# Attention pipelines whose TensorE order is written out, with the scores of two 64-row heads alternated

## The chip, the cores and the metric

The kernel runs on one core of a Trainium2 chip. The metric is device time in microseconds, the median of several executions of the whole program. Times inside the program come from one further execution, taken with the hardware profiler.

## The reference

Two transformer blocks of two layers each work on the same 512 tokens of width 1024, batch 1, in float32.

The first block, in each of its two layers, adds three branches: a multi-scale pooling branch, a gated causal convolution, and a dilated attention of 12 heads of width 64 in three dilation groups; then memory cross-attention and a gated feed-forward part. The second block has 256 context tokens beside the 512. Its first layer holds eight sliding-window heads of width 64 (two key heads, a sink each) and four differential heads, each with two softmaxes over queries and keys of width 64; its second layer is latent attention with 16 heads of 64 + 32 columns. A feed-forward part follows each. What matters here are the scores: a softmax over `q @ k.T` with 64 rows of contraction for the dilated, differential and window heads and 96 for the latent ones, its product with the values, and the projections from which q, k and v come.

```
sc = jnp.einsum("bhqd,bhqkd->bhqk", qb[g], kk).astype(jnp.float32) * scale   # dilated, hd = 64
p = jnp.exp(sc - m); o = jnp.einsum("bhqk,bhqkd->bhqd", p, vv) / den
```

## The kernel before

Float32 products are made of three matmuls on a high and a low part (`mm3`, lines 133 to 138: high by high, high by low, low by high); the lines 136, 137 and 138 therefore hold most matmuls of the program. `wload` (line 123) loads a weight unit with a DMA on the SP queue and splits it: ScalarE copies the high part (line 109), VectorE subtracts the low one (line 112).

Attention is done by `pipeline` (line 382), which is called three times: by `mix1` for the dilated heads (once in each layer of the first block), by `mix_ab` for the differential and then the window heads, and by `mix_mla` for the latent heads. A pipeline has items; an item is one head for one block of 128 queries and has four steps:

- `qk`: the scores of 128 queries against up to 768 columns into one of two PSUM buffers `S`, and their extreme value on VectorE (`nmax`, line 399, or 401 with a mask). The score matrix is negated, so the minimum is taken.
- `soft`: the exponential on ScalarE with the sum beside it (`exps`, line 411), the reciprocal on VectorE (416), and the scaling on GpSimd (`norm_probs`, 420). Differential heads combine two such results on VectorE (1061).
- `tr`: `probs_T` (line 422) transposes the probabilities on TensorE (line 430), three 128-column groups into each of two PSUM tiles `T`, of which there are two buffers; ScalarE copies the first tile out (109), VectorE the second (433).
- `pv`: the product with the values into a PSUM tile `p` (two buffers): `pv_pair` (line 444) for two heads of 64 columns at once, or line 1068 for a differential head.

`pipeline` emits, in each round i, step s of item i - steps[s], in the order `qk`, `tr`, `soft`, `pv`, and then filler. Filler (`Fill`, line 40) is a list of generators that emit other work in small steps and tell what each step should cost in nanoseconds; `run(ns)` hands out steps until the debt is paid, and stops at a tile's boundary when less than `hold` is left; `need(key)` runs everything up to that key at once. In `mix1` the filler is, in this order: the projections of the second pair of heads (`proj1`), the pooling branch's projections (`pool_in`, line 564, with a chain of sums on GpSimd in lines 576 and 578 and on VectorE in 584 to 586 behind each tile), the convolution branch (`conv_branch`, line 542) and the pooling branch's output (`pool_out`, line 591, which reads those sums). In `mix_ab` it is the projections `proj_ab` (line 1029) of the following heads; in `mix_mla` those of the following head group.

The program's instructions are ordered by the language's scheduler, which gives each engine the ready instruction that was emitted first, by its own idea of durations; the order on TensorE need not be that of the source. A projection (`tok_proj`, line 355) ends with copies by ScalarE, rotary steps on VectorE (lines 458 to 461, or `rope2`) and transposes (line 469, or `transposed`, line 1024) through the PSUM tiles `p`, each group of which is emptied by a ScalarE copy and a VectorE subtraction (line 120).

Two heads lie in one tile: rows 0 to 63 hold one, rows 64 to 127 the other. `items1` (dilated heads) has 16 items per layer, `diff_items` eight items per head, of which each pair shares a query block, and two context items, `window_items` 40, and the latent pipeline 64.

Of the kernel before, what the change touches and what calls it, by code (L numbers as in the profile page):

```python
# [39 lines left out]
class Fill:  # L40
# [28 lines left out]
    def drain(self):  # L69
        while self.gens:  # L70
            self._one()
# [7 lines left out]
class Net:  # L79
# [53 lines left out]
    def mm3(self, ps, l, r, first, last):  # L133

        mm = self.nc.tensor.matmul
        mm(ps, lhsT=l[0], rhs=r[0], start=first, stop=False)  # L136
        mm(ps, lhsT=l[0], rhs=r[1], start=False, stop=False)  # L137
        mm(ps, lhsT=l[1], rhs=r[0], start=False, stop=last)  # L138

    def gain(self, row):  # L140
        g = self.gp.tile([P, D], F32, name="g")
# [238 lines left out]


    def pipeline(self, items, fill, ns, steps=(0, 1, 2, 3)):
        for i in range(len(items) + steps[-1]):
            for s in (0, 2, 1, 3):
                j = i - steps[s]
                if 0 <= j < len(items) and items[j][s] is not None:
                    items[j][s]()
            fill.run(ns if isinstance(ns, (int, float)) else ns[min(i, len(items) - 1)])

    def ptile(self):  # L390
        self.turn = (self.turn + 1) % 6
# [83 lines left out]
        g["v"] = vt = self.work.tile([P, 4, 384], F32, name="vt", bufs=2)  # L475
        yield from self.tok_proj(hT, W[l, p, 2], range(4), 384, lambda t, ps: self.copy(vt[:, t], ps), tags=tags)

    def items1(self, p, g, fill, oT):

        mm = self.nc.tensor.matmul  # L480
        sh = {}
        out = []

        def item(b, h):
            st = {}
            rows = slice(64 * h, 64 * h + 64)
            qs = slice(b * P, (b + 1) * P)

            def qk():
                if (b, h) == (0, 0):  # L490
                    fill.need(p)
                q0, k0, q12, k12 = g["q0"], g["k0"], g["q12"], g["k12"]
                ps = self.psum("S")
                self.mm3(ps[:, 0], (q0[rows, 0, qs], q0[rows, 1, qs]), (k0[rows, 0], k0[rows, 1]), True, True)
                for j in range(2):
                    o = ps[:, 1, j * P : (j + 1) * P]
                    mm(o, lhsT=q12[rows, j, qs], rhs=k12[rows, j, qs], start=True, stop=True)
                st["s"] = ps.rearrange("p a b -> p (a b)")[:, :768]
                st["nm"] = self.nmax(st["s"], mask=self.mask1[:, b])

            def soft():
                st["P"], r = self.exps(st["s"], st["nm"], 768)
                self.norm_probs(st["P"], r)

            def tr():
                sh[b, h] = self.probs_T(st["P"], 6)

            def pv():
                v = g["v"]
                o = self.psum("p")[:, :P]  # L510

                def vs(hh, k):
                    c = hh * 64 + (max(k - 3, 0)) * P
                    return v[:, k if k < 4 else b, c : c + 64]

                self.pv_pair(o, [sh[b, 0], sh[b, 1]], vs)
                self.copy(oT[:, qs], o)

            return (qk, soft, tr, pv if h else None)

        return [item(b, h) for b in range(4) for h in range(2)]

    def shifts(self, dst, src, k):

# [87 lines left out]
    def mix1(self, l, hT, lead):  # L612
        nc, I = self.nc, self.I
        with ExitStack() as ctx:
            cf = ExitStack()
            with ExitStack() as c2:
                if l > 0:
                    self.ringctx.close()
                self.psum_pools(c2, S=2, T=2, p=2)
                if l == 0:  # L620
                    self.ready(1)
                    self.rope1()
                    self.consts1()
# [12 lines left out]
                self.masks1(self.pool(c2, "mask"))  # L636
                fp = self.pool(cf, "brf", 8, side="right")
                oF, aF, bF = ([fp.tile([P, 512], F32, name="brf") for _ in range(n)] for n in (2, 3, 3))
                fill.add(1, self.proj1(l, 1, hT, gs[1], ("p",)))
                fill.add("pool", self.pool_in(l, hT, pooled))  # L640
                fill.add("conv", self.conv_branch(l, hT, bF))
                fill.add("pool", self.pool_out(l, pooled, aF))
                self.pipeline(self.items1(0, gs[0], fill, oF[0]) + self.items1(1, gs[1], fill, oF[1]), fill, 7200, (0, 1, 2, 3))
                fill.drain()
            self.open_ring()
            mp = self.pool(ctx, "mT", KC)
# [401 lines left out]
            yield from self.transposed(src, col, range(4), g[n], s, tag=tags[-1])  # L1048
        g["v"] = v

    def diff_items(self, h, g, fill, oB):
# [20 lines left out]
        def item(t, m, first):  # L1072
            st = {}
            rows = slice(64 * m, 64 * m + 64)
            q = slice(t * P, (t + 1) * P)

            def qk():
                if first:
                    fill.need(h)
                qT, kT = g["a"], g["b"]  # L1080
                ql = (qT[rows, 0, q], qT[rows, 1, q])
                ps = self.psum("S")
                self.mm3(ps[:, 0], ql, (kT[rows, 0, :512], kT[rows, 1, :512]), True, True)
                self.mm3(ps[:, 1, :256], ql, (kT[rows, 0, 512:], kT[rows, 1, 512:]), True, True)
                st["s"] = ps.rearrange("p a b -> p (a b)")[:, :768]
                st["nm"] = self.nmax(st["s"])

            def soft():
                sh.setdefault(t, []).append(self.exps(st["s"], st["nm"], 768))
                if m:  # L1090
                    combine(t)

            def tr():
                sh["T", t] = self.probs_T(sh[t][0][0], 6)

            return (qk, soft, tr if m else None, (lambda: finish(t, 6)) if m else None)

        def ctx_item(t):
            st = {}
            q = slice(t * P, (t + 1) * P)  # L1100

            def qk():
                qT, kT = g["a"], g["b"]
# [12 lines left out]
            def tr():  # L1116
                sh["T", t] = self.probs_T(sh[t][0][0], 2)

            return (qk, soft, tr, lambda: finish(t, 2))

        return [item(t, m, t == 0 and m == 0) for t in range(4) for m in range(2)] + [ctx_item(t) for t in (4, 5)]

    def diff_T(self, oB, oT):

# [103 lines left out]
    def mix_ab(self, hT, lead):  # L1228
        nc, I = self.nc, self.I
        with ExitStack() as ctx:  # L1230
            with ExitStack() as c2:
# [34 lines left out]
            self.open_x(back)  # L1266
            self.open_xc()
# [444 lines left out]
```

## Time and profile before

| | us |
|---|---|
| median of 3 runs (lowest to highest) | 3593.13 (3589.31 to 3593.2) |
| the profiled execution | 3594.31 |
| its span in the trace | 3592.5 |
| TensorE busy in the span | 3519.9 (98%) |
| VectorE busy | 1917.2 (53%) |
| ScalarE busy | 1335.5 (37%) |
| GpSimd busy | 429.1 (12%) |
| DMA queue q1, share of 16 engines' span | 31.7% |
| pipeline of the dilated heads, first layer | 72.9 to 250.1 |
| pipeline of the dilated heads, second layer | 998.5 to 1175.9 |
| differential heads, then window heads | 1903.4 to 2231.4 |
| latent heads | 2948.4 to 3173.5 |

The trace names the engines PE (TensorE matmuls), PEld (its weight loads), DVE (VectorE), ACT (ScalarE), POOL (GpSimd) and SP (SyncE, which issues the DMAs). A matmul's duration reaches beyond the start of the next one, since they are pipelined; what a matmul costs is the distance between starts. `64*128` in a row is 64 rows by 128 columns of the array. A float32 matmul that is not split stands as two instructions. In a row's end, [x <-E tile line] is idle time of the engine before the instruction and what ended it.

### The profile page before, as it was taken

The numbers are of one execution on the slowest core, as the hardware profiler recorded it, in microseconds if no ns is written. First come the engines' busy times: TensorE is split into PE (matmuls) and PEld (weight loads), VectorE is DVE, ScalarE is ACT, GpSimd is POOL, SyncE is SP. The second block draws the span as 40 slices with busy tenths as digits, with TensorE's granted clock in tenths as the row PEclk, the third lists the DMA queues.
The fourth block names the chain that finished last, engine by engine and source line by source line (L and its number), as shares of the span: only waits on it lengthen the run. The fifth ranks groups of instructions, "written<-read, shape, count | busy, mean of one in ns | idle before, by whom it ended". The sixth has DMA issues, their size and how long they took to land.

```text
span 3592.5 us, 48260 instructions
## 1 busy us (share of the span) xinstructions
PE 3519.9 (98%) x19261; PEld 2994.1 (83%) x19261; DVE 1917.2 (53%) x3018; ACT 1335.5 (37%) x2372; POOL 429.1 (12%) x572
## 2 busy tenths in 40 slices
PE   8999999999999999999999999999999989999998
PEld 8877798888898778888878887888888878888887
DVE  4453357466534335666766666536663466753243
ACT  4432344332443324532344446332111356643222
POOL 0211111000102111200011122200000122220001
PEclk9999999999999999999999999999999999999999
DMA  4233334344322433354431112335443121022232
GB/s 129 83 129 94 100 112 141 106 144 135 103 66 93 135 94 124 121 167 150 131 107 40 36 48 77 125 93 168 132 132 103 46 80 33 25 89 87 90 102 86
DMA packets 110130, 364.02 MB, mean 101 GB/s; under 512 B 16617, under 2 KB 18209, under 8 KB 109905
## 3 DMA queue, kind: packets, MB, share of 16 engines
q1 hardware_dynamic: 109904, 360.94, 31.7%
q8 instruction: 151, 2.47, 0.3%
q14 instruction: 75, 0.61, 0.1%
HBM read 347.16 MB, written 13.73 MB: 100 GB/s over the span
## 4 chain that ended last, share of the span: by engine, by line
PE 90%; DVE 3%; ACT 2%; POOL 2%; DMA 1%; issue 1%; SPq 0%; ACTq 0%; POOLq 0%; DVEq 0%
PE ps L136 21%; PE ps L137 21%; PE ps L138 21%; PE p L136 4%; PE p L137 4%; PE p L138 4%; PE T L430 3%; PE p L444 3%; PE S L136 2%; PE S L137 1%; PE S L138 1%; DMA adaw<-in_ada_w_dram 1%; PE T L138 1%; PE T L136 1%; PE T L137 1%
## 5 line engine op out<-in xcount | busy, mean ns | idle before, releaser
L112 DVE TENSOR_TENSOR wlo<-raw,whi 128x1024 fp32r<-128x1024 f32 (+2 forms) x510 | 603.8, 1190 | 734.6 <-ACT whi L109 719.3
L109 ACT ACTIVATE whi<-raw 128x1024 fp32r<-128x1024 f32 (+2 forms) x510 | 518.1, 1019 | 1113.1 <-PE ps L137 710.2
L137 PE MATMUL ps<-hTlo,whi 128*128 128x512 f32 (+1 forms) x2048 | 757.6, 370 | 4.1 <-DVE hTlo L177 4.0
L136 PE MATMUL ps<-hThi,whi 128*128 128x512 f32 (+1 forms) x2048 | 757.7, 371 | 2.7 <-ACT hThi L109 1.4
L138 PE MATMUL ps<-hThi,wlo 128*128 128x512 f32 (+1 forms) x2048 | 756.7, 370 | 0.0
L136 PEld LDWEIGHTS ps<-hThi,whi 128*128 128x128 f32 x2048 | 385.8, 189 | 73.0 <-issue 3.5
L137 PEld LDWEIGHTS ps<-hTlo,whi 128*128 128x128 f32 x2048 | 386.5, 189 | 69.9 <-DVE hTlo L177 4.5
L138 PEld LDWEIGHTS ps<-hThi,wlo 128*128 128x128 f32 x2048 | 386.3, 189 | 65.2
L930 DVE SCALAR_TENSOR_TENSOR acc<-adaw,cs,acc 128x1024 f32<-128x1024 f32 x168 | 209.4, 1279 | 14.6 <-DMA adaw<-in_ada_w_dram 14.3
L136 PE MATMUL ps<-whi,a 128*128 128x512 f32 x440 | 170.9, 392 | 0.7 <-ACT a L109 0.7
L138 PE MATMUL ps<-whi,a 128*128 128x512 f32 x440 | 170.6, 390 | 0.0
L137 PE MATMUL ps<-wlo,a 128*128 128x512 f32 x440 | 170.6, 390 | 0.0
L136 PE MATMUL p<-whi,hThi 128*128 128x384 f32 x464 | 163.1, 352 | 7.5 <-ACT hThi L175 3.1
L137 PE MATMUL p<-wlo,hThi 128*128 128x384 f32 x464 | 158.2, 341 | 4.7 <-DVE wlo L112 4.7
L154 POOL TENSOR_SCALAR rstd<-ms 128x1 f32<-128x1 f32 x78 | 24.1, 309 | 1137.9 <-ACT junk L152 1122.7
L138 PE MATMUL p<-whi,hTlo 128*128 128x384 f32 x464 | 158.2, 341 | 0.7 <-DVE hTlo L112 0.7
L262 DVE TENSOR_TENSOR y<-y,ps 128x1024 f32<-128x1024 f32 x88 | 106.6, 1218 | 85.7 <-PE ps L138 85.4
L136 PE MATMUL ps<-whi,act 128*128 128x512 f32 x352 | 138.2, 395 | 0.0
L137 PE MATMUL ps<-wlo,act 128*128 128x512 f32 x352 | 137.2, 392 | 0.0
L138 PE MATMUL ps<-whi,act 128*128 128x512 f32 x352 | 136.3, 390 | 0.0
L420 POOL TENSOR_SCALAR g<-g,den 128x768 f32<-128x768 f32 (+3 forms) x88 | 74.6, 850 | 424.3 <-DVE den L416 375.6
L109 ACT ACTIVATE PT<-T 128x384 f32<-128x384 f32 (+2 forms) x160 | 74.4, 465 | 111.6 <-PE T L430 109.6
(407 smaller groups left out, 6830.8 us busy)
## 6 DMA issues: line engine op xcount, KB each, us to landing
raw<-in_ffn_w_dram SPq DMA_DIRECT2D x132, 512.0 KB
adaw<-in_ada_w_dram SPq DMA_DIRECT2D x96, 512.0 KB
raw<-in_w_up_dram SPq DMA_DIRECT2D x88, 512.0 KB
raw<-in_w_gate_dram SPq DMA_DIRECT2D x48, 512.0 KB
raw<-in_w_down_dram SPq DMA_DIRECT2D x44, 512.0 KB
raw<-in_w_qkv_dram SPq DMA_DIRECT2D x48, 384.0 KB
xd<-x SPq DMA_DIRECT2D x20, 512.0 KB
raw<-in_w_conv_dram SPq DMA_DIRECT2D x18, 512.0 KB
```

What stands on the lines that cost most here:

```text
L109: return self.nc.scalar.activation(out, in_, AF.Copy, scale=scale)
L112: return self.nc.vector.tensor_tensor(out, a, b, op=ALU.subtract)
L136: mm(ps, lhsT=l[0], rhs=r[0], start=first, stop=False)
L137: mm(ps, lhsT=l[0], rhs=r[1], start=False, stop=False)
L138: mm(ps, lhsT=l[1], rhs=r[0], start=False, stop=last)
L154: nc.gpsimd.tensor_scalar(r, ms, 1.0, EPS, op0=ALU.mult, op1=ALU.add)
L262: self.nc.vector.tensor_tensor(yps[t], yps[t], y, op=ALU.add)
L420: self.nc.gpsimd.tensor_scalar(Pt, Pt, r, 1.0, op0=ALU.mult, op1=ALU.mult)
L430: nc.tensor.transpose(ps[:, k * P : (k + 1) * P], Pt[:, (k0 + k) * P : (k0 + k + 1) * P], self.ident)
L444: self.nc.tensor.matmul(o[64 * h : 64 * h + 64], lhsT=vs(h, k), rhs=PTs[h][:, k], start=k == 0, stop=k == nk - 1)
L930: nc.vector.scalar_tensor_tensor(acc[r], w, c, acc[r], op0=ALU.mult, op1=ALU.add)
```

## The change

`pipeline` puts TensorE under a manual schedule: inside it, TensorE takes its instructions in the order in which the source emits them. The other engines are scheduled as before. The order in a round becomes `pv`, `qk`, `tr`, `soft`, then filler, and an item may bring its own step offsets. In `items1` and `diff_items`, the two heads of a tile become one item: their score matmuls are given out alternately (`mm3_two`), each head into its own `S` buffer, and then come two extremes, two exponentials and, in `items1`, 12 transposes in a row. In `mix1` the order of the filler becomes convolution, `pool_in`, `pool_out`; the second pair's projections are no filler any more but are emitted in one piece ahead of its first scores. In `mix_ab`, a head's projections are added to the filler only when the head before it begins. Window and latent items keep their steps.

```diff
+    def mm3_two(self, pss, ls, rs):
+        for i, j in ((0, 0), (0, 1), (1, 0)):
+            for ps, l, r in zip(pss, ls, rs):
+                self.nc.tensor.matmul(ps, lhsT=l[i], rhs=r[j], start=(i, j) == (0, 0), stop=i == 1)
...
     def pipeline(self, items, fill, ns, steps=(0, 1, 2, 3)):
-        for i in range(len(items) + steps[-1]):
-            for s in (0, 2, 1, 3):
-                j = i - steps[s]
-                if 0 <= j < len(items) and items[j][s] is not None:
-                    items[j][s]()
-            fill.run(ns if isinstance(ns, (int, float)) else ns[min(i, len(items) - 1)])
+        own = [it[4] if len(it) > 4 else steps for it in items]
+        with self.tc.manual_schedule(engines={mybir.EngineType.PE}):
+            for i in range(max(j + o[3] for j, o in enumerate(own)) + 1):
+                for s in (3, 0, 2, 1):
+                    for j, it in enumerate(items):
+                        if j + own[j][s] == i and it[s] is not None:
+                            it[s]()
+                fill.run(ns if isinstance(ns, (int, float)) else ns[min(i, len(items) - 1)])
...
-    def items1(self, p, g, fill, oT):
+    def items1(self, p, g, proj, oT):
...
             def qk():
-                if (b, h) == (0, 0):
-                    fill.need(p)
+                if b == 0 and p:
+                    drain(proj)
                 q0, k0, q12, k12 = g["q0"], g["k0"], g["q12"], g["k12"]
-                ps = self.psum("S")
-                self.mm3(ps[:, 0], (q0[rows, 0, qs], q0[rows, 1, qs]), (k0[rows, 0], k0[rows, 1]), True, True)
+                pss = [self.psum("S") for _ in both]
+                self.mm3_two([ps[:, 0] for ps in pss], [(q0[r, 0, qs], q0[r, 1, qs]) for r in both], [(k0[r, 0], k0[r, 1]) for r in both])
                 for j in range(2):
-                    o = ps[:, 1, j * P : (j + 1) * P]
-                    mm(o, lhsT=q12[rows, j, qs], rhs=k12[rows, j, qs], start=True, stop=True)
+                    for ps, r in zip(pss, both):
+                        mm(ps[:, 1, j * P : (j + 1) * P], lhsT=q12[r, j, qs], rhs=k12[r, j, qs], start=True, stop=True)
...
             def tr():
-                sh[b, h] = self.probs_T(st["P"], 6)
+                sh[b] = [self.probs_T(Pt, 6) for Pt in st["P"]]
...
-        return [item(b, h) for b in range(4) for h in range(2)]
+        return [item(b) for b in range(4)]
...
-                fill.add(1, self.proj1(l, 1, hT, gs[1], ("p",)))
+                proj = self.proj1(l, 1, hT, gs[1], ("p",))
+                fill.add("conv", self.conv_branch(l, hT, bF))
                 fill.add("pool", self.pool_in(l, hT, pooled))
-                fill.add("conv", self.conv_branch(l, hT, bF))
                 fill.add("pool", self.pool_out(l, pooled, aF))
-                self.pipeline(self.items1(0, gs[0], fill, oF[0]) + self.items1(1, gs[1], fill, oF[1]), fill, 7200, (0, 1, 2, 3))
+                items = self.items1(0, gs[0], None, oF[0]) + self.items1(1, gs[1], proj, oF[1])
+                self.pipeline(items, fill, [9000] * 4 + [8500] * 4, (0, 0, 1, 2))
...
             def qk():
-                if first:
+                if t == 0:
                     fill.need(h)
+                    fill.add(*after)
                 qT, kT = g["a"], g["b"]
...
+                pss = [self.psum("S") for _ in both]
+                for j, c, n in ((0, slice(0, 512), 512), (1, slice(512, 768), 256)):
+                    self.mm3_two([ps[:, j, :n] for ps in pss], ql, [(kT[r, 0, c], kT[r, 1, c]) for r in both])
...
-            return (qk, soft, tr if m else None, (lambda: finish(t, 6)) if m else None)
+            return (qk, soft, tr, lambda: finish(t, 6), (0, 0, 2, 3))
...
-                for i in range(1, 6):
-                    fill.add(i, self.proj_ab(hT, i, gs[i], ("p",)))
+                proj = [(i, self.proj_ab(hT, i, gs[i], ("p",))) for i in range(1, 6)]
                 items = []
                 for h in range(4):
-                    items += self.diff_items(h, gs[h], fill, oB[h])
+                    items += self.diff_items(h, gs[h], fill, oB[h], proj[h])
+                qk5 = items[-1][0]
+
+                def last():
+                    qk5()
+                    fill.add(*proj[4])
+
+                items[-1] = (last,) + items[-1][1:]
...
-                self.pipeline(items, fill, [3000] * n + [200] * (len(items) - n), (0, 1, 4, 5))
+                self.pipeline(items, fill, ([6000] * 4 + [3000] * 2) * 4 + [200] * (len(items) - n), (0, 1, 4, 5))
```

## Rows read from the trace of the kernel before

**Rows 1.** Windows view of four stretches: bounds, length, busy us (instructions) per engine, PEclk, DMA.

```profile
72.90:250.10 177.20, 174.46 (x1022) 148.59 (x1021) 79.70 (x159) 69.55 (x119) 32.03 (x44) 0.99 0.29 92
...
1903.40:2137.20 233.80, 229.25 (x1374) 203.59 (x1375) 148.07 (x365) 95.72 (x242) 38.19 (x67) 1.00 0.14 44
2137.20:2231.40 94.20, 92.58 (x750) 71.91 (x749) 67.08 (x257) 63.49 (x204) 33.09 (x54) 1.00 0.06 17
2948.40:3173.50 225.10, 222.04 (x1902) 195.11 (x1900) 157.93 (x333) 146.59 (x316) 60.03 (x64) 1.00 0.11 34
```

**Rows 2.** Timeline of TensorE around a lone head: start us, us, engine, line, operation, tiles, count.

```profile
1912.99 0.33 PE L137 MATMUL p<-wlo,hThi 128*128 128x384 f32 x1
1913.16 0.34 PE L138 MATMUL p<-whi,hTlo 128*128 128x384 f32 x1
1913.43 0.49 PE L136 MATMUL S<-qk 64*128 64x512 f32 x1
...
1914.67 0.44 PE L136 MATMUL p<-whi,hThi 128*128 128x384 f32 x1
1914.95 0.34 PE L137 MATMUL p<-wlo,hThi 128*128 128x384 f32 x1
```

**Rows 3.** Timeline of TensorE, two runs of six 256-column score matmuls.

```profile
1942.95 0.39 PE L136 MATMUL S<-qk 64*128 64x256 f32 x2
...
1943.51 0.60 PE L1068 MATMUL p<-v,PT 128*128 128x128 f32 x3
...
2142.27 0.38 PE L136 MATMUL S<-qk 64*128 64x256 f32 x1
...
2143.18 0.44 PE L430 MATMUL T<-ident,g 128*128 128x128 f32 x2
```

**Rows 4.** Timeline of TensorE, a head cut by two transposes.

```profile
97.88 0.39 PE L137 MATMUL S<-qk 64*128 64x512 f32 x1
98.20 0.44 PE L469 MATMUL p<-ident,tok 128*128 128x128 f32 x2
98.57 0.49 PE L138 MATMUL S<-qk 64*128 64x512 f32 x1
```

**Rows 5.** Timeline of all engines, three places with two T tiles or two maxima.

```profile
175.71 0.96 DVE L401 CUSTOM_DVE_ANT_0 S<-S,mask 128x768 f32<-128x768 f32 x1
...
1947.25 0.44 PE L430 MATMUL T<-ident,big 128*128 128x128 f32 x2 [0.56 <-ACT PT L109]
...
2130.38 0.73 DVE L401 CUSTOM_DVE_ANT_0 S<-S,mask 128x512 f32<-128x512 f32 x1
...
2132.20 0.55 DVE L433 COPY PT<-T 128x384 f32<-128x384 f32 x1
```

**Rows 6.** Timeline of all engines, the sums behind the last pool matmul.

```profile
173.62 0.69 DVE L112 TENSOR_TENSOR qk<-t,qk 128x512 fp32r<-128x512 f32 x1 [0.70 <-ACT qk L109]
...
174.44 0.57 ACT L109 ACTIVATE t<-p 128x512 f32<-128x512 f32 x1
...
182.21 0.75 DVE L586 SCALAR_TENSOR_TENSOR t<-t,poolc,t 128x512 f32<-128x512 f32 x1
```

**Rows 7.** Timeline of all engines, rotary steps of a projection tile.

```profile
106.69 0.49 ACT L109 ACTIVATE tok<-p 128x384 f32<-128x384 f32 x1 [4.61 <-PE p L138]
...
107.82 0.26 DVE L461 TENSOR_TENSOR tok<-ropeA,ropeB 128x96 f32<-128x96 f32 x1
```

**Rows 8.** Timeline of all engines, value products at the latent pipeline's end.

```profile
3164.68 1.53 PE L444 MATMUL p<-PT,v 128*64 128x128 f32 x24
...
3170.78 0.49 ACT L109 ACTIVATE PT<-T 128x384 f32<-128x384 f32 x1 [0.24 <-PE T L430]
...
3170.95 1.89 PE L444 MATMUL p<-PT,v 128*64 128x128 f32 x24
```

**Rows 9.** Windows view, a stall in the first layer and the stretch behind it.

```profile
126.00:129.00 3.00, 1.82 (x13) 1.40 (x11) 2.88 (x7) 1.99 (x5) 1.73 (x1) 1.00 0.31 42
129.02:132.43 3.41, 3.41 (x12) 3.03 (x12) 0.71 (x3) 1.62 (x4) 0.94 (x2) 0.50 0.28 115
```

More of the change, by code (lines that the diff above doesn't have):

```diff
@@ L482, in items1, with item @@
         out = []
-        def item(b, h):
+        def item(b):
             st = {}
-            rows = slice(64 * h, 64 * h + 64)
+            both = [slice(0, 64), slice(64, 128)]
             qs = slice(b * P, (b + 1) * P)
             def qk():
-                if (b, h) == (0, 0):
-                    fill.need(p)
+                if b == 0 and p:
+                    drain(proj)
                 q0, k0, q12, k12 = g["q0"], g["k0"], g["q12"], g["k12"]
-                ps = self.psum("S")
-                self.mm3(ps[:, 0], (q0[rows, 0, qs], q0[rows, 1, qs]), (k0[rows, 0], k0[rows, 1]), True, True)
+                pss = [self.psum("S") for _ in both]
+                self.mm3_two([ps[:, 0] for ps in pss], [(q0[r, 0, qs], q0[r, 1, qs]) for r in both], [(k0[r, 0], k0[r, 1]) for r in both])
                 for j in range(2):
-                    o = ps[:, 1, j * P : (j + 1) * P]
-                    mm(o, lhsT=q12[rows, j, qs], rhs=k12[rows, j, qs], start=True, stop=True)
-                st["s"] = ps.rearrange("p a b -> p (a b)")[:, :768]
-                st["nm"] = self.nmax(st["s"], mask=self.mask1[:, b])
+                    for ps, r in zip(pss, both):
+                        mm(ps[:, 1, j * P : (j + 1) * P], lhsT=q12[r, j, qs], rhs=k12[r, j, qs], start=True, stop=True)
+                st["s"] = [ps.rearrange("p a b -> p (a b)")[:, :768] for ps in pss]
+                st["nm"] = [self.nmax(s, mask=self.mask1[:, b]) for s in st["s"]]
             def soft():
-                st["P"], r = self.exps(st["s"], st["nm"], 768)
-                self.norm_probs(st["P"], r)
+                st["P"] = []
+                for s, nm in zip(st["s"], st["nm"]):
+                    Pt, r = self.exps(s, nm, 768)
+                    self.norm_probs(Pt, r)
+                    st["P"].append(Pt)
             def tr():
-                sh[b, h] = self.probs_T(st["P"], 6)
+                sh[b] = [self.probs_T(Pt, 6) for Pt in st["P"]]
             def pv():
@@ L514, in vs @@
                     return v[:, k if k < 4 else b, c : c + 64]
-                self.pv_pair(o, [sh[b, 0], sh[b, 1]], vs)
+                self.pv_pair(o, sh[b], vs)
                 self.copy(oT[:, qs], o)
-            return (qk, soft, tr, pv if h else None)
-        return [item(b, h) for b in range(4) for h in range(2)]
+            return (qk, soft, tr, pv)
+        return [item(b) for b in range(4)]
     def shifts(self, dst, src, k):
@@ L1049, in proj_ab, with diff_items @@
         g["v"] = v
-    def diff_items(self, h, g, fill, oB):
+    def diff_items(self, h, g, fill, oB, after):
         nc = self.nc
@@ L1070, in finish, with item @@
             nc.vector.scalar_tensor_tensor(oB[:, t], o, r, self.subln, op0=ALU.mult, op1=ALU.mult)
-        def item(t, m, first):
+        def item(t):
             st = {}
-            rows = slice(64 * m, 64 * m + 64)
+            both = [slice(0, 64), slice(64, 128)]
             q = slice(t * P, (t + 1) * P)
             def qk():
-                if first:
+                if t == 0:
                     fill.need(h)
+                    fill.add(*after)
                 qT, kT = g["a"], g["b"]
[L1081 to L1086, printed above, removed]
+                ql = [(qT[r, 0, q], qT[r, 1, q]) for r in both]
+                pss = [self.psum("S") for _ in both]
+                for j, c, n in ((0, slice(0, 512), 512), (1, slice(512, 768), 256)):
+                    self.mm3_two([ps[:, j, :n] for ps in pss], ql, [(kT[r, 0, c], kT[r, 1, c]) for r in both])
+                st["s"] = [ps.rearrange("p a b -> p (a b)")[:, :768] for ps in pss]
+                st["nm"] = [self.nmax(s) for s in st["s"]]
             def soft():
-                sh.setdefault(t, []).append(self.exps(st["s"], st["nm"], 768))
-                if m:
-                    combine(t)
+                sh[t] = [self.exps(s, nm, 768) for s, nm in zip(st["s"], st["nm"])]
+                combine(t)
             def tr():
                 sh["T", t] = self.probs_T(sh[t][0][0], 6)
-            return (qk, soft, tr if m else None, (lambda: finish(t, 6)) if m else None)
+            return (qk, soft, tr, lambda: finish(t, 6), (0, 0, 2, 3))
         def ctx_item(t):
@@ L1117, in tr @@
                 sh["T", t] = self.probs_T(sh[t][0][0], 2)
-            return (qk, soft, tr, lambda: finish(t, 2))
-        return [item(t, m, t == 0 and m == 0) for t in range(4) for m in range(2)] + [ctx_item(t) for t in (4, 5)]
+            return (qk, soft, tr, lambda: finish(t, 2), (0, 0, 2, 3))
+        return [item(t) for t in range(4)] + [ctx_item(t) for t in (4, 5)]
     def diff_T(self, oB, oT):
```

## The prediction

> **What bounds the kernel now.** I read the windows of the pipelines first. TensorE is busy for 174.5 of 177.2 us in the first layer's pipeline, 229.3 of 233.8 in the four differential heads, 92.6 of 94.2 in the window heads, 222.0 of 225.1 in the latent ones, and its clock is full [rows 1]; VectorE, next, has 63 to 71% in the last three. So time is won only by fewer TensorE slots, and each new idle stretch of TensorE is paid in full: no slack hides it. Then I followed TensorE's timeline start to start, since the durations overlap; and last, around its transposes, what else was queued.
>
> **What becomes cheaper.** A lone head's six score matmuls take 1.24 us (1913.43 to 1914.67). The matmul ahead of them is followed after 0.27 instead of the 0.17 between its neighbours, the first behind them after 0.28: two changes between 128 and 64 rows, 0.21 beside the block, 1.45 us in all [rows 2]. What alternation is worth, this kernel shows by chance: six 256-column matmuls that came alternately from the two row halves take 0.56 us, six from one half 0.91 [rows 3]. The three saved slots are whole (0.12 each), so the second of a pair is nearly free. A pair of heads then costs what one costs now: 1.4 us less. There are 16 pairs in the differential heads (4 heads, 4 blocks) and 16 in the two layers (2 x 2 x 4), whose heads have the same three 512-column matmuls and two small ones: 32 x 1.4 = 45 us. Bounds: nothing shows it at 512 columns; if those did not overlap, three slots of 0.23 a pair were lost, 22 us; the upper end is 45. I take 45, the rows' own mechanism.
>
> The scheduler now cuts score blocks apart. Two transposes between the second and third matmul of one head put the third 0.69 behind the second, where 0.23 and two transposes at 0.11 would do, and the next block again pays for its entry: 0.3 to 0.4 us a cut [rows 4]. Along the four stages I count 44 such cuts of scores or value products; in source order they go: 44 x 0.35 = 15 us. Idle time that goes with the old order: about 8 us, and the two stretches of 3.4 us in the two layers in which the clock fell to half behind an idle 1.2 us (one in [rows 9]), some 3 us. **Saved: 71 us.**
>
> **What becomes dearer**, because TensorE may no longer pass a waiting instruction:
>
> 1. *Twelve transposes in a row* (probs_T of both heads, four T tiles, two T buffers). The third tile waits for ScalarE's copy of the first: 0.56 us in one of the few such places [rows 5]. The fourth waits for VectorE's copy of the second, and that copy is queued behind both maxima of the scores just given out. Such a case is there too: a second maximum starts at 2130.38 and the copy at 2132.20 only. Two maxima of 768 columns (0.96 each, with their readouts about 2.1), the copy (0.55) and 0.1 of hand-over put the fourth tile 2.75 us behind the scores, instead of 1.0: 1.75 a pair, 14 pairs, and 0.5 for the two last ones: 25 us. Bounds: 0.56 x 16 = 9, if the copy gets ahead of the second maximum; 32, if VectorE is also found inside a weight split each time. I take 25: the maxima are emitted ahead of the copy, and the only case shown goes that way.
>
> Here the Trainium skill has a rule against the change (TensorEngine Tiling (Array Packing), Performance Considerations): packing makes TensorE faster but not the emptying of PSUM, which may become the limit. By it the 25 stands; without it, by the ScalarE wait alone, the sum below would be 16 less.
>
> 2. *pool_out straight behind pool_in.* Filler by its own costs: nine convolution tiles and three pool tiles are 96 steps of 648, and by the pipeline's seventh round 61,500 are dealt, 95 steps. Step 96 and pool_out's seven so fall into the eighth. From the copy of the last pool tile to its scaled sums it takes from 174.44 to 182.96, then a split (ScalarE, and VectorE's 0.69): 10 us [rows 6]; ahead of the first matmul that needs them stand four steps, 2.7 us. 7 to 9 idle, twice: 16 us. Today the convolutions hide that chain. Lower bound: 4, if the eighth round's transposes came behind step 96.
>
> 3. *The second projection drained in one piece* for p = 1: the last tile's copy and rotary steps end 1.4 us after they start [rows 7], and the third group of transposes waits for a buffer through a copy and a split (0.57 and 0.69 for 512 columns [rows 6], with hand-overs 1.6, less the 0.44 of the four transposes between), 1.2. Both for q and k, in both layers: 10 us (0 to 14).
>
> 4. *The same in the differential heads*: four groups of transposes through two buffers, each emptied by a copy and a split: two such waits of 0.7 (two groups are half as wide) and 0.8 for engines that are busy with the scores, an estimate; 2.2 us for each of five projections, 11 us (5 to 15).
>
> 5. *Value products right behind their own transposes.* With the order 3, 0, 2, 1 only the filler stands between. At the very end that happens now: the products take 1.89 instead of 1.53, waiting for a copy of 0.49 [rows 8]: 0.36, on idle engines. Window heads have hardly any filler (20 pairs at 0.5), the latent heads none for 19 of 32 (at 0.45): 18 us (14 to 30).
>
> 6. Refilling the pipeline where differential heads give way to window heads, and smaller buffer waits: 9 us (4 to 14), an estimate by the same copies.
>
> 7. *Clock.* Idle stretches of 1.2 us were followed by 3.4 us at half clock, in which half the work is done [rows 9], while the 0.56 was not: that stretch kept its clock [rows 1, 5]. pool_out's two waits surely do it: 2 x 1.7; one or two more: 5 us (3 to 20).
>
> **Lost: 94 us**, of it some 27 in each layer, which saves 17. No added DMA; the weights come in another order (convolutions ahead of projections) through the same queue, at 29% of its engines' time or less [rows 1], so I charge nothing; without that cover, one 512 KB load a layer at that stretch's 92 GB/s, 6 us each. Scores need both S buffers at once: the next pair comes a filler of 6 to 9 us later, two maxima and two exponentials take 4, so nothing there.
>
> **Sum.** The profiled execution took 3594.3 us, 1.2 above the median of the runs shown: 3594.3 - 71 + 94 = 3617, against the median 3616.
>
> **Rivals.**
> *Faster, the queues give way.* The scheduler knows TensorE's fixed order and could put first, on VectorE, ScalarE and GpSimd, what TensorE waits for. Item 1 falls to 9, 2 to 10, 3 and 4 to 12, 5 to 14, 6 and 7 to 6: 51 lost, 20 won, 3574; with half of these again, 3560. It decides once the losses are below 71. For it: ScalarE and VectorE have idle time everywhere [rows 1]. Against it: the copy at 2132.20 [rows 5] stood behind work that TensorE did not wait for. Chance 0.35.
> *No change*: losses of 64 to 78, between the two. 0.12.
> *No overlap at 512 columns*, so that the change half fails to do what it says: 22 us more, 3640. The even lag in [rows 3] speaks against it; 0.05.
> *Slower as summed*: 0.48.
>
> **Numbers.** Likeliest is slower, 3616. About 0.2% (7 us) is what a measurement of this kernel can tell from no change. Slower 0.48 + 0.05 = 0.53, same 0.12, faster 0.35. Of the unknown costs the lower ends give a loss of 39 and the upper ones 143; not all fall on one side. The range goes down to 3560, which leaves out a tenth among the faster cases, and up to 3648 for the missing overlap or the clock. The forecast's own range is 3601 to 3640.
>
> **What would show it.** Right: S matmuls of the pairs start in twos a few ns apart and their blocks take 1.2 to 1.3 us; T idle for 1 us or more behind L401 in the two layers; one idle stretch of 7 us or more ahead of pool_out, with the clock at half behind it; L444 waiting for PT in the window and latent heads; both layers' pipelines longer than 177 us, the differential heads shorter. Wrong: layers shorter than 170 us, or T waits of 0.5 only; then the faster rival holds.

## The result and the profile after

The changed kernel takes 3679.49 us (median; 3674.76 to 3682.88) against 3591.58 of the kernel before beside it: a ratio of 1.0244, 95% interval 1.0227 to 1.0262. It is slower by 88 us. The forecast was 3616, and 3679 lies above its range.

The profiled execution has a span of 3679.9 us against 3592.5, 87.4 more. The four pipelines hold all of it, as the windows of the changed kernel show (bounds, length, busy us and instructions of PE, PEld, DVE, ACT and POOL, granted clock, DMA share, GB/s); the third row holds both parts of the differential and window stage.

```profile
71.60:268.70 197.10, 169.46 (x1022) 144.18 (x1021) 79.47 (x161) 68.63 (x120) 30.94 (x44) 0.95 0.26 81
1017.60:1216.80 199.20, 172.10 (x1021) 146.50 (x1021) 77.72 (x159) 67.80 (x117) 28.90 (x40) 0.94 0.24 74
1948.10:2286.40 338.30, 316.43 (x2122) 276.34 (x2122) 218.42 (x621) 162.53 (x443) 68.15 (x120) 0.94 0.11 35
3002.40:3259.80 257.40, 232.35 (x1896) 202.05 (x1896) 160.62 (x330) 148.17 (x312) 57.78 (x64) 0.97 0.09 28
```

The same four stages of the kernel before, over the same work:

```profile
72.90:249.90 177.00, 174.26 (x1021) 148.56 (x1021) 79.70 (x159) 69.55 (x119) 31.92 (x43) 0.99 0.29 91
998.50:1175.20 176.70, 174.25 (x1021) 148.38 (x1021) 78.56 (x158) 69.18 (x116) 31.32 (x40) 0.99 0.28 88
1903.40:2230.10 326.70, 321.44 (x2121) 275.50 (x2122) 214.73 (x621) 158.33 (x443) 71.27 (x120) 1.00 0.11 35
2949.70:3172.60 222.90, 221.18 (x1896) 194.74 (x1896) 156.60 (x330) 145.22 (x312) 60.03 (x64) 1.00 0.11 33
```

Everywhere the distance between length and PE's busy time has grown, and the clock is no longer full. Each stage splits into three parts. *Idle* is length less PE busy. *Clock* is half of the busy time that lies in stretches whose granted clock is 0.50, since about half the work is done there (e5 and e11 below: 176 matmuls against 323 in 41 us); these stretches sum to 95.6 us in the four stages, against 6.8 before. *Rest* is what is left: the matmuls as they would go at full clock, with the waits too short to show beside a running matmul.

| stage, us | length before, after | idle | clock | rest |
|---|---|---|---|---|
| dilated heads, layer 1 | 177.0, 197.1 | 2.7, 27.6 | 1.7, 7.9 | 172.6, 161.5 |
| dilated heads, layer 2 | 176.7, 199.2 | 2.4, 27.1 | 1.7, 11.0 | 172.5, 161.1 |
| differential, window | 326.7, 338.3 | 5.3, 21.9 | 0, 16.3 | 321.4, 300.1 |
| latent | 222.9, 257.4 | 1.7, 25.1 | 0, 6.0 | 221.2, 226.3 |
| sum | 903.3, 992.0 | 12.2, 101.7 | 3.4, 41.2 | 887.7, 849.1 |

So the matmuls did become cheaper, by 39 us, idle time cost 89 and the clock 38. What TensorE waits for, from the list of its waits (us in total, times, longest):

```profile
PE T L439 <- ACT PT L109: 33.5, 32, 3.0
PE p L136 <- ACT qk L109: 12.6, 2, 6.5
PE p L1037 <- DVE qk L120: 10.7, 9, 2.0
...
PE p L1037 <- DVE hClo L120: 7.1, 3, 2.8
PE p L453 <- DVE kTlo L112: 6.4, 3, 2.1
PE p L478 <- DVE tok L470: 5.5, 4, 1.4
PE p L1037 <- DVE kTlo L112: 4.7, 2, 2.7
...
PE p L478 <- ACT qk L109: 4.1, 4, 1.4
...
PE p L453 <- ACT tok L109: 2.5, 3, 1.0
```

From the top: the twelve transposes, pool_out, the groups of transposes of the differential projections, the two projections in one piece (L478), and in the latent stage (hClo, kTlo, tok) transposes and value products that wait for a `p` buffer. The first in detail, from the timeline of all engines behind one pair's scores:

```profile
84.00 0.87 PE L439 MATMUL T<-ident,g 128*128 128x128 f32 x6
84.10 0.97 DVE L410 CUSTOM_DVE_ANT_0 S<-S,mask 128x768 f32<-128x768 f32 x1 [3.28 <-PE S L506]
84.58 0.49 ACT L109 ACTIVATE PT<-T 128x384 f32<-128x384 f32 x1 [4.53 <-PE T L439]
...
84.98 1.00 DVE L410 CUSTOM_DVE_ANT_0 S<-S,mask 128x768 f32<-128x768 f32 x1
...
85.22 0.52 PE L439 MATMUL T<-ident,yg 128*128 128x128 f32 x3 [0.34 <-ACT PT L109]
...
85.90 0.55 DVE L442 COPY PT<-T 128x384 f32<-128x384 f32 x1
...
86.59 0.55 PE L439 MATMUL T<-ident,yg 128*128 128x128 f32 x3 [0.85 <-ACT PT L109]
```

VectorE's copy of the second tile (85.90) stands behind both maxima (84.10, 84.98), so the fourth tile starts 2.59 us behind the first, as forecast from [rows 5]. The last row names ScalarE, but the fourth tile takes the second one's buffer: what it waited for is the copy of 85.90, which ends at 86.45, 0.14 ahead of it, as the copy of 84.58 ends 0.15 ahead of the third tile.

### The profile page after: what moved, and what is told of

It is laid out like the page before. It is cut to its first block, busy times and chain, and to the rows that moved or that the text cites. A ratio compares the mean times of both kernels' runs of the same rounds, so it can differ in the third digit from the quotient of the medians.

```text
span 3679.9 us, 48287 instructions
## 1 busy us (share of the span) xinstructions
PE 3519.7 (96%) x19261; PEld 2996.1 (81%) x19261; DVE 1923.9 (52%) x3018; ACT 1341.4 (36%) x2372; POOL 419.4 (11%) x572
## 4 chain that ended last, share of the span: by engine, by line
PE 80%; DVE 5%; ACT 3%; issue 2%; POOL 2%; DMA 1%; SPq 0%; ACTq 0%; POOLq 0%; DVEq 0%
PE ps L136 20%; PE ps L137 20%; PE ps L138 20%; PE p L136 3%; PE p L137 3%; PE p L138 3%; PE p L453 2%; PE T L439 2%; PE S L136 1%; DVE wlo L112 1%; PE S L137 1%; PE S L138 1%; DMA adaw<-in_ada_w_dram 1%; PE p L1081 1%; PE S L144 1%
```

## The experiments

The first four ask whether the order, its sequence or the pairs cost the time.

**e1**, pairs with the order left to the scheduler, in all pipelines:

```
-        with self.tc.manual_schedule(engines={mybir.EngineType.PE}):
+        with ExitStack():
```

> The changed kernel with its pairs and its new dealing of filler, but TensorE's order left to the scheduler in all four pipelines. Theory (the fixed order exposes waits and these lower the clock; the pairs themselves are a gain): 3545 to 3570 us, TensorE's granted clock 0.99 or more in each pipeline, the waits for T and p buffers mostly gone. Rival 1 (two S buffers taken at once cost what alternation gains): 3590 to 3610. Rival 2 (the filler's new order is the cause: pool_out behind pool_in, the projection in one piece): it stays above 3620, since these two are still there.

3609.6 us, ratio 1.0051 (1.0036 to 1.0066): 70 less than the changed kernel, still 18 more than before. That is rival 1's range, but not by its cause: in the layers and the third stage TensorE waits for an `S` buffer (for an exponential) only 0.8 us in all. Its windows, second layer left out:

```profile
72.50:250.40 177.90, 163.45 (x1022) 139.03 (x1021) 78.88 (x160) 67.98 (x120) 30.45 (x42) 0.98 0.28 89
...
1905.90:2240.80 334.90, 323.50 (x2121) 279.28 (x2122) 216.74 (x621) 160.66 (x443) 68.55 (x120) 0.93 0.11 35
2956.00:3184.90 228.90, 225.28 (x1896) 195.62 (x1896) 158.46 (x330) 145.88 (x312) 57.91 (x64) 1.00 0.10 32
```

The fixed order costs 19 and 21 us in the layers and 28 in the latent stage. In the layers TensorE is busy 11 us less than before, and idle 12 more: pool_out still waits 6.1 in each. So far rival 2 is right: this wait comes of the filler's new order, stays without the fixed one, and is gone with the old dealing (e5). In the differential and window stage 22 us are lost to the clock, nearly all in one stretch of 41 us at half. The latent stage is 6 us above before's 223 with nothing changed in it but the sequence in which a round's functions are called, by which the other engines' queues are filled.

**e2**, transposes first:

```
-                for s in (3, 0, 2, 1):
+                for s in (3, 2, 0, 1):
```

> The changed kernel, still in a fixed order, but in each round the transposes stand ahead of the scores instead of behind them. Theory: the copies of the T tiles are no longer queued behind the two maxima of the scores just given out (0.7 us for each of 16 pairs) and the next value products no longer stand right behind their own transposes (0.4 for some 40 pairs in the window and latent heads), with the clock that goes with it: 25 to 45 us less, 3635 to 3655. Rival (the time is in the long waits: group transposes, pool_out, evacuations of projections): less than 10 us, 3670 to 3685.

3657.3 us, 22 less than the changed kernel and 2 above the theory's range. Layers 190 and 192, latent 247; as the theory has it: in the layers the waits for T fall from 31.9 us in 28 to 15.5 in 18. In the differential and window stage nothing is won: the rest falls by 7, idle by 5, but the clock takes 29.7 instead of 16.3.

**e3**, the fixed order left out in the latent pipeline alone:

```
-                    self.pipeline(items, fill, 2600, (0, 1, 3, 4))
+                    self.pipeline(items, fill, 2600, (0, 1, 3, 4), free=True)
```

> The changed kernel, with TensorE's order left to the scheduler in the latent pipeline alone, where nothing is paired and the filler is as it was. Theory: that pipeline goes back from 258 us to 224 and all else stays: 3645 (3640 to 3650). Rival (the latent pipeline is slower for what stands before it, weights that arrive later or a changed start): 3670 or more.

3649.7 us, 30 less, by the theory. The latent row is e1's to 0.1 us:

```profile
3000.70:3229.50 228.80, 225.21 (x1895) 195.55 (x1896) 158.41 (x330) 145.84 (x312) 57.83 (x64) 1.00 0.10 32
```

Idle fell from 25.1 to 3.6, the clock's loss from 6.0 to nothing: 27.5 of the 28.6 us won are these two, so both come of the fixed order.

**e4**, pairs head by head:

```
-        for i, j in ((0, 0), (0, 1), (1, 0)):
-            for ps, l, r in zip(pss, ls, rs):
+        for ps, l, r in zip(pss, ls, rs):
+            for i, j in ((0, 0), (0, 1), (1, 0)):
```

> The changed kernel, the three 512-column and 256-column score matmuls of a pair given out head by head instead of alternately, all else the same. Theory (what alternation saves is TensorE time on the path): 0.8 us more for each 512-column block of 32 pairs and 0.45 for the 256-column one of 16, 30 to 40 us, 3710 to 3720. Rival (the saving only lengthens the wait for the T tiles behind the scores, since the first head's maximum starts earlier when it goes first): 0 to 12 us more, 3680 to 3692.

3678.5 us, no change. But not for the rival's reason. TensorE's timeline of e4 at the first pair:

```profile
72.13 0.97 PE L144 MATMUL S<-qk 64*128 64x512 f32 x6
72.92 0.61 PE L506 MATMUL S<-qk 64*128 64x128 f32 x8
73.47 0.50 PE L136 MATMUL p<-hThi,whi 128*128 128x512 f32 x1
```

and of the changed kernel:

```profile
71.58 0.96 PE L144 MATMUL S<-qk 64*128 64x512 f32 x6
72.38 0.61 PE L506 MATMUL S<-qk 64*128 64x128 f32 x8
72.91 0.50 PE L136 MATMUL p<-hThi,whi 128*128 128x512 f32 x1
```

Six matmuls of 512 columns take 0.79 and 0.80 us. Given out three of one half and then three of the other, they still ran in twos (starts at 72.126 and 72.136, 72.462 and 72.472, 72.693 and 72.703). The records don't name the half; but the starts within a two are 10 ns apart here and 3 to 4 in the changed kernel, so the order did change, and six of one half take 0.91 us even at 256 columns [rows 3]. That the two heads stand next to each other is enough; alternation adds nothing.

The next four take the parts that e1 left.

**e5**, e1 with the layers' filler and the latent sequence of before:

```
-                proj = self.proj1(l, 1, hT, gs[1], ("p",))
-                fill.add("conv", self.conv_branch(l, hT, bF))
+                fill.add(1, self.proj1(l, 1, hT, gs[1], ("p",)))
                 fill.add("pool", self.pool_in(l, hT, pooled))
+                fill.add("conv", self.conv_branch(l, hT, bF))
                 fill.add("pool", self.pool_out(l, pooled, aF))
...
-                self.pipeline(items, fill, [9000] * 4 + [8500] * 4, (0, 0, 1, 2))
+                self.pipeline(items, fill, 14400, (0, 0, 1, 2))
...
-                    self.pipeline(items, fill, 2600, (0, 1, 3, 4))
+                    self.pipeline(items, fill, 2600, (0, 1, 3, 4), (0, 2, 1, 3))
```

> The kernel e1 (pairs, order left to the scheduler) with two things put back: in the two layers the filler is dealt as before the change (second projection, pool_in, convolutions, pool_out), and in the latent pipeline the functions of a round are called in the old sequence. Theory (in e1 the gain of the pairs in the layers was eaten by the wait of 6.1 us for pool_out and its half clock): the layers fall from 177.8 us each to 162 to 168, the latent pipeline from 228.9 to 223, in all 3572 to 3582. Rival (pairs bring nothing in the layers, since both maxima then come at once and the T tiles wait for them): the layers stay at 174 or more, in all 3595 to 3605.

3585.4 us, ratio 0.9985 (0.9975 to 0.9994), 3 above the theory's upper end. The layers take 169.1 and 168.7 at full clock, the latent stage 223.3. What is left is the third stage, and in it this (windows; last row: the stretch at half clock alone):

```profile
1887.00:2221.10 334.10, 323.45 (x2121) 279.44 (x2122) 216.25 (x621) 161.04 (x443) 68.56 (x120) 0.93 0.11 35
...
2105.00:2146.00 41.00, 41.00 (x176) 31.83 (x176) 17.53 (x65) 16.57 (x47) 7.36 (x10) 0.50 0.00 1
```

Ahead of it TensorE waited twice, by its timeline:

```profile
2098.87 0.66 PE L1037 MATMUL p<-ident,tok 128*128 128x128 f32 x4 [1.20 <-DVE qk L120]
...
2104.22 0.66 PE L439 MATMUL T<-ident,big 128*128 128x128 f32 x4 [1.24 <-POOL big L429]
```

**e8**, e5 with that stage's projections handed to the filler at once:

```
-                proj = [(i, self.proj_ab(hT, i, gs[i], ("p",))) for i in range(1, 6)]
+                for i in range(1, 6):
+                    fill.add(i, self.proj_ab(hT, i, gs[i], ("p",)))
```

> e5, and in the stage of the differential and window heads the projections too are handed to the filler at once, as before the change, instead of one per head. Theory (there the last projection, dealt in one piece, makes TensorE wait 1.2 us several times, after which e1 ran 41 us at half clock): no long stretch at half clock, this stage falls from 335 us to 303 to 315, in all 20 to 30 us less than e5. Rival (the clock falls from the pairs themselves or from the window heads' small matmuls): the stage stays at 325 or more and the long stretch is still there.

3601.0 us, 15 more than e5: the theory fails, and the outcome is the rival's. The stage takes 352.4, with 61 us on end at half clock:

```profile
2110.00:2171.00 61.00, 59.06 (x237) 42.33 (x237) 24.41 (x90) 22.23 (x63) 10.57 (x17) 0.50 0.03 9
```

The rival's reason, the pairs or the window heads by themselves, falls with e11 below, which has both. Dealing decides, but before's dealing, made for single heads, is not the one that suits pairs.

**e6**, e8 with e4's edit:

> e8 with the 512-column and 256-column score matmuls of a pair given out head by head. Under the fixed order (e4) that cost nothing. Theory (there the saved time went into the wait behind the scores; with an order in which TensorE can do other work in that wait it shows): 0.8 us for each of 32 blocks of 512 columns and 0.45 for 16 of 256, so 20 to 33 us more than e8. Rival (alternation saves no time anywhere, the chain from scores through maxima to T tiles sets the end): within 6 us of e8.

3600.2 us, as e8: by the free order too, alternation saves nothing. The first pair's scores start in twos here as well (73.200 and 73.210).

**e7**, the changed kernel with matmuls of no use in the long waits (this in `transposed`; likewise 8 in `proj1` and 50 in `pool_out`):

```
             yield 0.0
+            self.keep_busy(6)
             ps = self.psum(tag)
```

> The changed kernel in its fixed order, with 128-column matmuls of no use put where TensorE waits longest: 6 ahead of each group of transposes in the projections, 8 in the layers' projection, 50 ahead of pool_out; they write spare columns of a scores buffer. They take some 0.11 us each, 55 to 60 us in all, against some 45 us of waits at these places. Theory (the change loses more by the half clock, 100 us more of it than before, than it does by the waits themselves): less time at half clock, and 20 to 40 us less in all although TensorE does more: 3640 to 3660. Rival (the waits are what costs, the low clock mostly lies within them): 3690 to 3710.

3713.8 us, 34 more; the theory's number fails, and 3 above the rival's range. There were 824 of them at 0.112 us, 92 us and not 60. By the same split the rest grew by 91 us, while idle fell from 101.7 to 66.2 and the time at half clock in the stages from 95.6 to 47.8. The time at half clock does fall with the waits, but this way of filling them costs more than it returns.

The last ones work on the third stage and the latent order.

**e9**, pairs in the layers alone (`diff_items` and `mix_ab` of before, the rest of e5):

```
-        return [item(t) for t in range(4)] + [ctx_item(t) for t in (4, 5)]
+        return [item(t, m, t == 0 and m == 0) for t in range(4) for m in range(2)] + [ctx_item(t) for t in (4, 5)]
...
-                self.pipeline(items, fill, ([6000] * 4 + [3000] * 2) * 4 + [200] * (len(items) - n), (0, 1, 4, 5))
+                self.pipeline(items, fill, [3000] * n + [200] * (len(items) - n), (0, 1, 4, 5), (0, 2, 1, 3))
```

> The kernel before, with pairs in the two layers alone (as in e5: TensorE's order left to the scheduler, filler dealt as before the change); the stage of the differential and window heads and the latent pipeline are those of before. Theory (pairs are a gain wherever no wait and no half clock come with them): the layers 169 us each as in e5, the other pipelines 327 and 223 as before, no long stretch at half clock: 16 us under the kernel before, 3573 to 3577. Rival (e5's small gain was mostly chance or the layers give it back behind the pipeline): 3583 to 3590.

3578.7 us, ratio 0.9961 (0.9948 to 0.9973): faster than before, by 13, where the theory had 16. Its first layer and its third stage:

```profile
71.70:240.80 169.10, 162.46 (x1021) 138.79 (x1021) 79.25 (x159) 68.94 (x119) 30.38 (x44) 1.00 0.30 94
...
1889.00:2215.70 326.70, 321.43 (x2122) 275.56 (x2122) 214.65 (x621) 158.16 (x443) 71.01 (x120) 1.00 0.11 36
```

The second layer takes 169.0. There is no half clock in either layer.

**e10**, e5 with useless matmuls where differential heads give way to window heads (this in the window heads' `tr`; likewise 8 ahead of each group of the last projection):

```
             def tr():
+                if t == 0 and c < 2:
+                    self.keep_busy(10)
                 sh[t, c, kv] = self.probs_T(st["P"], nk)
```

> e5 with matmuls of no use (128 columns, 8 ahead of each group of transposes of the last projection, 10 ahead of the transposes of the first four window heads, 72 in all, about 8 us) where the differential heads give way to the window heads. Theory (the 41 us at half clock there, which cost some 20 us, set in behind TensorE's waits of 1.2 us at this place): with the waits filled the long stretch is gone or short, 3566 to 3578. Rival (the window heads' small matmuls bring the clock down by themselves, or the added matmuls cost as much): the stretch stays, 3588 to 3595.

3582.9 us: the stretch of 41 us at half clock shrinks to 6.8, which gives back 19 us (22.0 to 3.4); the rest grew by 20, 16 of it the 144 matmuls (0.112 us each, twice as many as I had counted). The mechanism is the theory's, the gain is not.

**e11**, e5 with the last two projections dealt during the fourth differential head:

```
-                    items += self.diff_items(h, gs[h], fill, oB[h], proj[h])
+                    items += self.diff_items(h, gs[h], fill, oB[h], proj[h : h + 1] if h < 3 else proj[3:])
...
-([6000] * 4 + [3000] * 2) * 4
+([6000] * 4 + [3000] * 2) * 3 + [11000] * 4 + [5000] * 2
```

> e5 with the last two projections both handed out during the fourth differential head (11000 and 5000 a round instead of 6000 and 3000), so that the last one is not done in one piece with no head in flight. Theory (the clock falls where TensorE has only transposes and refilling heads to do): no long stretch at half clock, the stage falls from 334 to 310 to 318, 3562 to 3572. Rival (the window heads reach their low clock in any case): the stage stays above 328, 3582 to 3592.

3568.8 us, ratio 0.9935 (0.9921 to 0.9949), the best: 23 under the kernel before, 111 under the changed one. Its third stage, and the stretch that answers to e5's 41 us:

```profile
1888.50:2205.80 317.30, 308.90 (x2121) 266.85 (x2122) 216.48 (x621) 159.51 (x443) 69.02 (x120) 0.99 0.11 37
...
2110.00:2151.00 41.00, 40.41 (x323) 31.75 (x322) 28.30 (x104) 27.00 (x76) 12.49 (x17) 1.00 0.01 1
```

In 41 us TensorE got through 323 matmul instructions instead of 176, and the two waits of 1.2 us ahead are gone: its longest from 2064 to 2151 is 0.6.

**e12**, the fixed order with the latent scores ahead of the value products:

```
-                    self.pipeline(items, fill, 2600, (0, 1, 3, 4))
+                    self.pipeline(items, fill, 2600, (0, 1, 3, 4), (0, 3, 2, 1))
```

> The changed kernel in its fixed order, in the latent pipeline alone each round gives out the scores ahead of the value products instead of behind them. Theory (in the fixed order the value products stand right behind the filler's projection, whose two p buffers are not yet emptied, and right behind their own transposes; 0.4 us in some 20 places and waits of 1 to 2 us in six): the latent pipeline falls from 257 to 235 to 245, 3658 to 3668. Rival (its waits are those of the transposes and projections for each other's evacuations, which stay): 253 or more, 3674 or more.

3671.9 us, 8 less, between the two. The latent stage takes 248.3: rest 8.7 less and idle 5.4 less, but 5 more to the clock. The first are the value products that stood behind their own transposes: start to start, those of the stage (L453) take 49.5 us instead of 57.6. The waits for `p` buffers stayed (hClo 6.6, kTlo 4.7 and 5.6).

**e13**, e11 with the fixed order in the differential and window stage:

```
-+ [200] * (len(items) - n), (0, 1, 4, 5))
++ [200] * (len(items) - n), (0, 1, 4, 5), fixed=True)
```

> e11 with TensorE's order fixed again in the stage of the differential and window heads alone. Theory (two separate losses: the fixed order adds waits there, some 10 us, and the value products right behind their own transposes; and waits of 1 us or more in a row bring the clock down, whatever the dealing): the stage goes from 317 to 330 to 345 us with 20 us or more at half clock, 3580 to 3596. Rival (with the last projections dealt in time the fixed order costs no more than a free one there): 320 or less, 3566 to 3573.

3589.1 us, 20 more than e11; the theory. The stage goes from 317.3 to 340.6: idle 15.8 more, the clock 11.7 more (34 us at half instead of 7), the rest 4.2 less.

```profile
1885.40:2226.00 340.60, 316.41 (x2122) 276.00 (x2122) 218.03 (x621) 161.64 (x443) 68.28 (x120) 0.95 0.11 34
```

Not tried: the fixed order with the layers' old dealing. There the second projection would wait for `qk` buffers that only scores further back in TensorE's order set free.

## Why the prediction was wrong

The direction was right, and the cause in the main: a fixed order turns hand-overs into waits, and these outweigh the pairs. Letting the order go gave 70 us back (e1), the old dealing in the layers and the old call sequence in the latent heads another 24 (e5). The forecast was a loss of 23 on the trace, 87 came. By the table's columns it said idle +63 (items 1 to 4 and 6, less the old 8), clock +2, rest -42; measured were +89, +38 and -39.

**The step that failed is item 7, the clock**: "pool_out's two waits surely do it: 2 x 1.7; one or two more: 5 us (3 to 20)". It cost 41. I had two stalls with half clock behind them (one in [rows 9]) and charged the two largest new ones and one or two more. In the changed kernel the stages have 17 stretches at half clock. The two at pool_out (6.8 us each) cost 5 us by the split, not far from the 3.4 charged; the other 15, spread over all four stages, cost 36. The longest of them began during the second of these two waits, by the timeline of the changed kernel:

```profile
2170.29 0.87 PE L1037 MATMUL p<-ident,tok 128*128 128x128 f32 x6 [0.96 <-DVE v L1050]
2172.36 1.12 PE L1037 MATMUL p<-ident,tok 128*128 128x128 f32 x4 [1.20 <-DVE qk L120]
```

and the window of the stretch that goes with it:

```profile
2171.50:2192.00 20.50, 17.24 (x76) 13.70 (x76) 10.77 (x38) 9.43 (x29) 4.85 (x9) 0.50 0.18 62
```

Which stall pays is not told by its length. The waits of 0.34 and 0.85 between the transposes at 84 us left the clock at 1.00, but so did 1.40 and 1.19 in a row (147.66 and 149.59) and 2.78 (3145.43), while a lone 2.48 (192.23) had 3.4 us at half clock with it. The same wait of 1.79, of the same transposes a head apart, did both:

```profile
2038.30 1.93 PE L1037 MATMUL p<-ident,tok 128*128 128x128 f32 x6 [1.79 <-DVE qk L120]
...
2086.40 0.44 PE L1037 MATMUL p<-ident,tok 128*128 128x128 f32 x2 [1.79 <-DVE qk L120]
```

with these windows behind them:

```profile
2038.30:2041.70 3.40, 3.27 (x14) 2.78 (x15) 2.26 (x5) 0.98 (x2) 0.15 (x1) 0.50 0.41 116
...
2086.50:2092.00 5.50, 4.81 (x36) 3.74 (x36) 3.12 (x8) 1.85 (x6) 0.79 (x3) 1.00 0.25 74
```

What decides is open; a price of stalls has to be a wide range for each stage, and not a count of the largest.

**The second is item 6**, "smaller buffer waits: 9 us (4 to 14), an estimate". The latent stage alone has 20.7 (7.1 + 6.4 + 4.7 + 2.5 in the list of waits), and e3 shows that they go with the fixed order. I had looked for value products behind their own transposes there, not for the filler's products and transposes holding both `p` buffers.

The other terms came near in size, some of them by luck. *Pairs*, 45: e9's layers fell in the rest by 10.1 and 10.0, e5's third stage by 20.0 (e11's by 15.7), 40 us for 32 pairs, 1.25 each. The reason was half wrong: [rows 3] show alternation, but adjacency does it (e4, e6). The Trainium skill (TensorEngine Tiling (Array Packing), Tiling Modes) states that different tiles can run weight loads and matmuls in parallel. It gives no order for them there; e4's 0.79 us for six agrees. *Cuts*, 15: not measured apart; in the latent heads without their late value products the rest is 3.6 under before's (e12). *Item 1*, 25: 31.9 in the layers. Eight of the 16 pairs show the chain forecast, at 1.2 us each and not 1.75, 9.8 in all; most of the other 22 fell on pairs whose copies also stood behind a weight split or the pooling branch's sums, up to 3.01 and 2.14 in one pair (224.91 and 227.56), so that the sum came near by luck. There the prediction leaned on the rule of the Trainium skill that packing does not speed up the emptying of PSUM (same page, Performance Considerations). By itself it doesn't give the 25: with the same packing in a free order each layer waits 3.8 us for T (e9) instead of 16. e2, which takes the copies out from behind the maxima, left one pause of 0.34 where the pair shown has 0.34 and 0.85. *Item 2*, 16: 12.6 in two waits, but 12.2 of it stay in e1, where TensorE may pass; the dealing costs it, not the fixed order. *Item 3*, 10: 9.6 (L478). *Item 4*, 11: 10.7 in 9 waits, of which 6.5 stay in e1. *Item 5*, 18: its latent half was 19 x 0.45 = 8.6, and e12 won 8.7 in the rest; the window half was not measured apart.

The rival that the queues give way is refuted by the timeline at 85.90 (its 3560 doesn't follow from its own terms: half of its 51 lost would give 3547); the missing overlap by 0.80 us for six. Of the signs named, T idle, pool_out's wait (6.5 and 6.1 us, not 7) and both layers above 177 us came; the missing one was how much of each stage would run at half clock.

## What to carry to other kernels

Two heads that each use half of the array's rows need only stand next to each other in TensorE's order (0.79 us for six 512-column matmuls). A fixed order is worth its price only where every wait behind it has been looked at: here it lost in each stage (19 and 21 us in the layers, 28 in the latent heads, 23 in e13), while the same pairs in a free order, with the filler dealt so that no stage changes hands without work beside it, won 23. Where stalls of about a microsecond or more are added, charge the half clock behind them as its own term, stage by stage, and in a wide range: here it was 38 us of the 88, and waits of one length had it behind them in one place and not in another.

## What was not expected of the hardware

A low clock can stay although TensorE is never idle: in e5 it was busy for 41.00 of 41.00 us at 0.50 (1.2 of 2.4 GHz), in e8 for 59.06 of 61.00, while work of the same kind ran at 1.00 in the kernel before [rows 1] and in e11. In e5 it fell behind waits of 1.20 and 1.24 us where the window heads begin, and filling these (e10) left 6.8 us of it. What brought it back up in the end the runs don't show, nor why of two waits of 1.79 us one had half clock behind it and one had not. And score matmuls start in twos 10 ns apart even where three of one row half are given out ahead of three of the other.
